# The first expert chosen on the chip, fewer places, and high-half products ahead of low ones

## The chip, the cores and the metric

The kernel runs on one core of one Trainium2 chip. The metric is the device time of one execution in microseconds (us). TensorE multiplies, VectorE and ScalarE convert and copy, GpSimd does some subtractions and indirect transfers, and SP issues the loads of weights to the core's 16 DMA engines. Each engine takes its instructions in program order.

## The reference

Two transformer layers over 512 tokens of width 1024: sliding-window attention with a dense SwiGLU, then forgetting attention with a mixture of eight experts, of which each token uses two. The stage that matters here:

```python
    logits = (x2 @ w_router).astype(jnp.float32) + b_router.astype(jnp.float32)
    top_vals, top_idx = lax.top_k(logits, TOP_K)
    gates = jax.nn.softmax(top_vals, axis=-1)
...
    def expert_block(args):
        xb, e = args
        h = xb @ w_in[e]
        return (jax.nn.silu(h[:, :D_FF]) * h[:, D_FF:]) @ w_out[e]
```

D_FF is 2816. An expert's weights are 1024 x 5632 and 2816 x 1024 numbers of 4 bytes, 34.6 MB; all eight are read once.

## The kernel before

**Weights.** The class `Weights` keeps a list of chunks of about 1 MB (128 x 2048 floats) in the order of use; an expert has 33, the last one 34. A chunk goes through three steps. `load` issues its DMA on SP into one of the raw buffers (three, and four "deep" ones once attention has given up its memory). `upper` lets ScalarE write its fp16 high half `wh` (L149), in two pieces of 1048 and 1000 columns. `lower` lets VectorE write the fp16 low half `wl` (L158) from the raw data and `wh`, after which the raw buffer is free and `load` goes on. Seven pairs of `wh` and `wl` exist; `free` says which were used up. `tick`, called between groups of matmuls, does a piece or two of each. `need` forces a chunk to be there. Every product is three matmuls: high weight by high data, high by low, low by high.

**Experts.** The kernel gives each of eight slots a fixed number of places, `CAP`. Slot 0 always has expert 0, whose weights can be loaded before anything is routed; the others are sorted by their tokens (`order_of`: `key`, `slot`, `ose`) and put on slots 1 to 7 by `TURN`, and SP reads their numbers from `eid` (`exp_of`, L296). A loop at the end (`nit`) serves tokens for which a slot has no place; `full` and `over` count whether there are any. A slot's places are the columns of its matmuls. `block4` computes four blocks of 128 hidden features for one unit of two chunks (L1442 to L1444), `quad` takes the products out, `gate_pair` does the last two blocks, `down_wide` the way down (L1471 to L1473); the last slot uses `down_direct`.

**Hand-over.** The last layer's attention ends with `finish`: four tiles of 128 tokens go through the output product, residual and norm. `aside(t, h, k)` hooks routing work between its matmuls: `route` computes a tile's logits, `ranks` the two best experts of each token, `places_of` each token's place in its expert's list and the one-hot lists of slot 0 (L1224), and `choose` gathers slot 0's token rows by matmuls of those one-hots (L1237, L1241). Of the last tile, `turn1` transposes the rows (L394), then `route`, `ranks`, `places_of` and `choose` follow, `chosen_to` copies the rows into `XA` (L231 on ScalarE, L1569 on VectorE) and slot 0 starts. Three chunks of expert 0 are loaded and converted during attention.

**Chores.** `small_work` is a list of small jobs: the lists of places (`lists`), the gates (`gates`, `gate_parts`) and a scaling of `xtok`. Each `tick` in slot 0 does one, from its first unit on.

## Time and profile before

| | us |
|---|---|
| median of three runs (1633.46 to 1636.43) | 1633.89 |
| the profiled execution | 1634.23 |
| its span, first to last instruction | 1632.4 |
| TensorE busy | 1578.6 |
| VectorE busy | 1210.9 |
| ScalarE busy | 950.3 |
| experts' first product at | 788.91 |

Times in the rows are counted from the start of the span. The view of the chain that ended last is no help in this kernel: it names only the last scatter. So the views read are the busy time of stretches, the waits, and the timeline.

### The profile page before, as it was taken

What the parts mean: (1) busy time and instruction counts of PE and PEld (TensorE: products, weight loads), DVE (VectorE), ACT (ScalarE), POOL (GpSimd) and SP (SyncE); (2) the same over time, 40 slices, a digit from 0 to 9 for tenths busy, and PEclk for the clock granted to TensorE, in tenths of its full rate; (3) what the DMA queues carried; (4) which work ended last, traced back from release to release, by engine and by line L of the source; (5) the groups of instructions that cost most, each with busy time, mean ns of one, the idle gap of its engine ahead of it and who ended that gap; (6) DMA issues with size and microseconds to landing.
All of it is one profiled execution on the core that took longest, in us unless ns stands there. A gap on an engine that the chain in (4) does not pass through costs nothing. (4 is left out here: it accounts for less than half of the span.)

```text
span 1632.4 us, 42978 instructions
## 1 busy us (share of the span) xinstructions
PE 1578.6 (97%) x18640; PEld 1267.8 (78%) x18640; DVE 1210.9 (74%) x1811; ACT 950.3 (58%) x1447; POOL 267.7 (16%) x264
## 2 busy tenths in 40 slices
PE   7998999999999999999899999999999999999996
PEld 6775654444444747765899999999999999999984
DVE  6798543333634568787898798888979889699997
ACT  6676243333211356663676787767877678666773
POOL 0443100000200000003120330203112030130251
PEclk9999999999999999999999999999999999999998
DMA  7511043332631132201899899999999999999993
GB/s 275 178 53 53 27 129 104 103 104 91 219 114 60 53 129 92 66 27 65 308 363 364 293 394 377 352 370 305 390 357 361 375 320 373 329 297 360 358 369 113
DMA packets 180549, 370.16 MB, mean 227 GB/s; under 512 B 6589, under 2 KB 49597, under 8 KB 180352
## 3 DMA queue, kind: packets, MB, share of 16 engines
q1 hardware_dynamic: 173280, 343.48, 58.6%
q0 software_dynamic: 4768, 15.47, 4.0%
q10 hardware_dynamic: 2304, 8.39, 1.4%
q8 instruction: 148, 2.42, 0.6%
q14 instruction: 49, 0.40, 0.1%
HBM read 355.08 MB, written 12.39 MB: 225 GB/s over the span
## 5 line engine op out<-in xcount | busy, mean ns | idle before, releaser
L158 DVE SCALAR_TENSOR_TENSOR wl<-raw,wh 128x1048 f16<-128x1048 f32 (+3 forms) x658 | 794.7, 1258 | 100.3 <-ACT wh L149 100.1
L149 ACT ACTIVATE wh<-raw 128x1048 f16<-128x1048 f32 (+3 forms) x658 | 641.8, 1036 | 101.7 <-PE bk L239 42.9
L1444 PE MATMUL bk<-xa,wl 128*128 128x160 f16 (+3 forms) x1280 | 260.0, 231 | 0.9 <-DVE wl L158 0.9
L1442 PE MATMUL bk<-xa,wh 128*128 128x160 f16 (+3 forms) x1280 | 260.1, 231 | 0.8 <-ACT xa L231 0.8
L1443 PE MATMUL bk<-xa,wh 128*128 128x160 f16 (+3 forms) x1280 | 260.0, 231 | 0.0
L1443 PEld LDWEIGHTS <-wh 128*128 128x128 f16 x2560 | 250.5, 98 | 3.6 <-issue 2.4
L1444 PEld LDWEIGHTS <-wl 128*128 128x128 f16 x2560 | 250.5, 98 | 1.3 <-DVE wl L158 1.1
L1442 PEld LDWEIGHTS <-wh 128*128 128x128 f16 x2560 | 250.4, 98 | 0.7
L1473 PE MATMUL bk<-act,wl 128*128 128x160 f16 (+6 forms) x1232 | 235.3, 227 | 1.2 <-DVE wl L158 1.2
L1472 PE MATMUL bk<-act,wh 128*128 128x160 f16 (+6 forms) x1232 | 235.3, 227 | 0.0
L1471 PE MATMUL bk<-act,wh 128*128 128x160 f16 (+6 forms) x1232 | 235.2, 227 | 0.0
L1442 PE MATMUL bk<-xe,wh 128*128 128x128 f16 (+2 forms) x1280 | 223.2, 221 | 2.2 <-DVE sa L1458 1.4
L1443 PE MATMUL bk<-xe,wh 128*128 128x128 f16 (+2 forms) x1280 | 223.1, 221 | 0.0
L1444 PE MATMUL bk<-xe,wl 128*128 128x128 f16 (+2 forms) x1280 | 223.1, 221 | 0.0
L237 PE MATMUL bk<-xTh,wh 128*128 128x512 f16 (+2 forms) x656 | 204.8, 322 | 1.2 <-DVE Kx L234 0.9
L239 PE MATMUL bk<-xTh,wl 128*128 128x512 f16 (+2 forms) x656 | 204.6, 322 | 1.4 <-DVE wl L158 1.4
L238 PE MATMUL bk<-xTl,wh 128*128 128x512 f16 (+2 forms) x656 | 204.6, 322 | 0.5 <-DVE xTl L234 0.5
L1460 POOL TENSOR_TENSOR act<-sa,act 128x512 f16<-128x512 f32 (+6 forms) x40 | 106.3, 2659 | 284.7 <-ACT act L231 284.6
L239 PEld LDWEIGHTS <-wl 128*128 128x128 f16 x944 | 92.4, 98 | 49.0 <-DVE wl L158 2.9
L237 PEld LDWEIGHTS <-wh 128*128 128x128 f16 x944 | 92.4, 98 | 48.7 <-ACT wh L149 2.0
L238 PEld LDWEIGHTS <-wh 128*128 128x128 f16 x944 | 92.5, 98 | 46.6 <-issue 1.5
L1473 PEld LDWEIGHTS <-wl 128*128 128x128 f16 x1232 | 120.5, 98 | 1.6 <-DVE wl L158 1.6
(349 smaller groups left out, 2669.2 us busy)
## 6 DMA issues: line engine op xcount, KB each, us to landing
raw<-in_w_exp_in_dram SPq DMA_DIRECT2D x176, 1024.0 KB
raw<-in_w_exp_out_dram SPq DMA_DIRECT2D x85, 1024.0 KB
raw<-in_w_ffn_in_dram SPq DMA_DIRECT2D x22, 1024.0 KB
raw<-in_w_out_dram SPq DMA_DIRECT2D x8, 1024.0 KB
raw<-in_w_ffn_out_dram SPq DMA_DIRECT2D x8, 1024.0 KB
raw<-in_w_in_fox_dram SPq DMA_DIRECT2D x8, 1024.0 KB
raw<-in_w_in_swa_dram SPq DMA_DIRECT2D x4, 896.0 KB
raw<-in_w_mem_kv_dram SPq DMA_DIRECT2D x3, 1024.0 KB
```

The source lines that it names most:

```text
L149: self.nc.scalar.activation(h[:, p:e], t[:, p:e], AF.Copy, scale=SW)
L158: self.nc.vector.scalar_tensor_tensor(l, src, SW, h, op0=OP.mult, op1=OP.subtract)
L237: nc.tensor.matmul(o, lh, rh, start=first, stop=False, **kw)
L238: nc.tensor.matmul(o, lh, rl, start=False, stop=False, **kw)
L239: nc.tensor.matmul(o, ll, rh, start=False, stop=last, **kw)
L1442: nc.tensor.matmul(o, wh[:, k, c], xe[0][:, k, :C], start=first, stop=False, skip_group_check=True)
L1443: nc.tensor.matmul(o, wh[:, k, c], xe[1][:, k, :C], start=False, stop=False, skip_group_check=True)
L1444: nc.tensor.matmul(o, wl[:, k, c], xe[0][:, k, :C], start=False, stop=k == KD - 1, skip_group_check=True)
L1460: lambda: nc.gpsimd.tensor_sub(act[1][:, j, :C], sa[:, :, :C], act[0][:, j, :C])]
L1471: nc.tensor.matmul(o, wh[:, k, c], act[0][:, kk, :C], start=first, stop=False, skip_group_check=True)
L1472: nc.tensor.matmul(o, wh[:, k, c], act[1][:, kk, :C], start=False, stop=False, skip_group_check=True)
L1473: nc.tensor.matmul(o, wl[:, k, c], act[0][:, kk, :C], start=False, stop=kk == KF - 1, skip_group_check=True)
```

## The change

Slot 0's expert is now chosen on the chip: after three of the four tiles are routed, `choice` counts their tokens, takes the expert with the second most (ties by number), and keeps its one-hot `oh0` and its number `e0i`. Expert loads are shut (`shut`) until then, and SP reads `e0i` ahead of the first. `CAP` falls by four in five slots. The one-hots of slot 0 need `oh0` and move to `first_list`, after the last tile's norm; `choose` moves behind it. Four pieces of `upper` are forced between `route` and the second part of `choose`. The first two units of slot 0 do all their products with high weights first (`passes` (0, 1), through `need_high`) and then those with low weights (2). `lists` runs at once, the other chores only from the fourth unit on (`calm`); the gates are split in two, and the count of tokens without a place becomes a chore (`beyond`). Lists and gates of slot 0 move to later units.

```diff
@@ -51,7 +51,7 @@
 PIECE = 1048
-CAP = [160, 128, 152, 134, 144, 140, 168, 128]
+CAP = [156, 128, 148, 130, 140, 136, 168, 128]
 TURN = [0, 6, 2, 5, 3, 4, 1, 7]
@@ -92,6 +92,7 @@
         self.piece = PIECE
+        self.shut = True
@@ -107,6 +108,8 @@
             i = self.dma - self.from_
+            if i >= 0 and self.shut:
+                return
             pool, back = self.raw, NRAW
@@ -173,6 +176,11 @@
+    def need_high(self, i):
+        while self.hcut <= i:
+            assert self.upper(True)
+        return self.chunks[i][3][0]
     def free(self, u, n=None):
@@ -289,11 +297,12 @@
-    expert = {0: 0}
+    expert = {}
...
         if s not in expert:
-            expert[s] = nc.sync.value_load(eid[0:1, s:s + 1], min_val=0, max_val=NEXP - 1)
+            row = eid[0:1, s:s + 1] if s else e0i[0:1, 0:1]
+            expert[s] = nc.sync.value_load(row, min_val=0, max_val=NEXP - 1)
         return exp_src(expert[s])[which]
@@ -355,7 +364,6 @@
         nc.vector.tensor_scalar(R["first"], R["iota8"], -1.0, None, op0=OP.mult)
-        nc.vector.memset(R["first"][:, 0:1], FAR * NEXP)
         R["room"] = base.tile([128, NEXP, NT], FT, name="room")
@@ -1169,6 +1177,10 @@
     selb = base.tile(V3, BF, name="selb")
+    oh0 = base.tile([128, NEXP], FT, name="oh0")
+    low0 = base.tile([128, 1], FT, name="low0")
+    e0i = base.tile([128, 1], I32, name="e0i")
+    pos0 = base.tile([128, NT], FT, name="pos0")
@@ -1211,6 +1223,21 @@
+    def choice(pb):
+        for i in range(NT - 1):
+            nc.tensor.matmul(pb[:, 64:64 + NEXP], ones, selb[:, i, :], start=i == 0, stop=i == NT - 2)
+        key0 = small.tile([128, NEXP], FT, name="key0")
+        nc.vector.scalar_tensor_tensor(key0, pb[:, 64:64 + NEXP], float(NEXP), iota8, op0=OP.mult, op1=OP.add)
+        most = small.tile([128, NEXP], FT, name="most")
+        nc.vector.max(out=most, in_=key0)
+        nc.vector.tensor_scalar(oh0, key0, most[:, 1:2], None, op0=OP.is_equal)
+        cross(key0, oh0, iota8, OP.mult)
+        nc.vector.tensor_reduce(low0, key0, axis=AX.X, op=OP.add)
+        nc.vector.tensor_copy(e0i, low0)
+        W.shut = False
+        W.load()
     def places_of(t0, t1, pb):
@@ -1220,8 +1247,15 @@
               pb[:, 32 + t0 * NEXP:32 + t1 * NEXP].rearrange("p (t e) -> p t e", e=NEXP), OP.add)
+    def first_list(t0, t1):
+        n = t1 - t0
+        own = small.tile([128, NT, NEXP], FT, name="own")[:, :n]
+        cross(own, posm[:, t0:t1], oh0[:, None, :].to_broadcast([128, n, NEXP]), OP.mult)
+        nc.vector.tensor_reduce(pos0[:, t0:t1], own, axis=AX.X, op=OP.add)
         for t in range(t0, t1):
-            nc.vector.tensor_scalar(oh_[0][:, t, :CAP[0]], iota_c[:, :CAP[0]], posm[:, t, 0:1], None, op0=OP.is_equal)
+            nc.vector.tensor_scalar(oh_[0][:, t, :CAP[0]], iota_c[:, :CAP[0]], pos0[:, t:t + 1], None, op0=OP.is_equal)
@@ -1268,10 +1302,11 @@
             oh_.append(op.tile([128, NT, CMAX], FH, name="PTh", bufs=2))
-            places_of(0, 3, bank())
+            pb3 = bank()
+            choice(pb3)
+            places_of(0, 3, pb3)
         if (t, h, k) == (3, 1, 15):
             xe_out.extend([bank2(), bank2(), bank()])
-            choose(range(0, 6), range(3))
@@ -1303,13 +1338,17 @@
     finish(u_o1, mixT, gb1, out_left, turn1, aside)
+    first_list(0, NT - 1)
     turn1(NT - 1)
-    choose(range(6, 11), range(3))
+    choose(range(0, 8), range(3))
     pb = bank()
     route(NT - 1, pb)
-    choose(range(11, 2 * KD), range(3))
+    for _ in range(4):
+        W.upper(True)
+    choose(range(8, 2 * KD), range(3))
     ranks(NT - 1, NT, *rank_tmp())
     places_of(NT - 1, NT, pb)
+    first_list(NT - 1, NT)
     for i in range(NT):
@@ -1430,22 +1469,24 @@
-    def block4(C, u, xe, b, tick):
-        wh, wl = unit(u, 512)
+    def block4(C, u, xe, b, tick, passes=(0, 1, 2)):
+        ws = unit(u, 512)
         for kk in (0, 4):
...
                 for k in range(kk, kk + 4):
-                    first = k == 0 and f % 2 == 0
-                    nc.tensor.matmul(o, wh[:, k, c], xe[0][:, k, :C], start=first, stop=False, skip_group_check=True)
-                    nc.tensor.matmul(o, wh[:, k, c], xe[1][:, k, :C], start=False, stop=False, skip_group_check=True)
-                    nc.tensor.matmul(o, wl[:, k, c], xe[0][:, k, :C], start=False, stop=k == KD - 1,
-                                     skip_group_check=True)
+                    for p in passes:
+                        if p < 2 and 2 not in passes:
+                            w = W.need_high(W.first[u] + kk // 4)[:, k % 4 * 512 + f * 128:k % 4 * 512 + f * 128 + 128]
+                        else:
+                            w = ws[p == 2][:, k, c]
+                        nc.tensor.matmul(o, w, xe[p == 1][:, k, :C], start=p == 0 and k == 0 and f % 2 == 0,
+                                         stop=p == 2 and k == KD - 1, skip_group_check=True)
                 if f % 2:
                     tick()
-            if kk == 0:
+            if kk == 0 and 2 in passes:
                 W.free(u, 1)
@@ -1551,13 +1592,17 @@
     tot = small_t("tot", [128, 1])
-    nc.vector.scalar_tensor_tensor(key, pb[:, 64:64 + NEXP], float(NEXP), first, op0=OP.mult, op1=OP.add)
-    nc.vector.max(out=top, in_=key)
-    cross(over, top[:, :, None].to_broadcast([128, NEXP, NT]), full, OP.is_gt)
-    nc.vector.tensor_reduce(tot, over.rearrange("p a b -> p (a b)"), axis=AX.X, op=OP.add)
-    nc.vector.tensor_copy(toti, tot)
+    def beyond():
+        nc.vector.max(out=top, in_=key)
+        cross(over, top[:, :, None].to_broadcast([128, NEXP, NT]), full, OP.is_gt)
+        nc.vector.tensor_reduce(tot, over.rearrange("p a b -> p (a b)"), axis=AX.X, op=OP.add)
+        nc.vector.tensor_copy(toti, tot)
     def order_of():
+        nc.vector.scalar_tensor_tensor(key, oh0, FAR * NEXP, first, op0=OP.mult, op1=OP.add)
+        nc.vector.scalar_tensor_tensor(key, pb[:, 64:64 + NEXP], float(NEXP), key, op0=OP.mult, op1=OP.add)
         nc.vector.tensor_copy(cnt, pb[:, 64:64 + NEXP])
@@ -1600,6 +1645,8 @@
         nc.scalar.activation(gt[:, 0], gt[:, 0], AF.Exp)
+    def gates_of():
         nc.vector.tensor_scalar(gt[:, 1], gt[:, 0], 1.0, None, op0=OP.add)
@@ -1622,11 +1669,14 @@
     def small_work():
-        lists()
-        yield
         gates()
         yield
+        yield
+        gates_of()
+        yield
         gate_parts()
+        yield
+        beyond()
         yield
@@ -1640,9 +1690,9 @@
     chores = small_work()
-    next(chores)
-    pend = []
+    lists()
+    pend, calm = [], []
@@ -1651,7 +1701,8 @@
             pend.pop(0)()
-        next(chores, None)
+        if calm:
+            next(chores, None)
         W.tick(1 if W.hcut >= W.done + LEAD else 2)
@@ -1737,27 +1788,35 @@
                     sa = mx.tile([128, 4, CMAX], FT, name="sa", bufs=2)
-                b = bank2()
-                block4(C, u, XE[s], b, tick)
+                if (s, i) == (0, 0):
+                    ahead = [bank2(), bank2()]
+                    for v, b in zip(u_ei[s], ahead):
+                        block4(C, v, XE[s], b, lambda: None, (0, 1))
+                if s == 0 and i < 2:
+                    b = ahead[i]
+                    block4(C, u, XE[s], b, tick, (2,))
+                else:
+                    b = bank2()
+                    block4(C, u, XE[s], b, tick)
                 rest = quad(C, b, i % 2, sa, act, i // 2)
...
             pend.extend(rest)
+            if (s, i) == (0, 3):
+                calm.append(True)
+            if (s, i) == (0, 9):
+                G[0] = own_gates(0, oh0_, bank())
             if (s, i) == (0, 2):
-                for _ in range(2):
-                    next(chores, None)
-                G[0] = own_gates(0, oh, bank())
-            if (s, i) == (0, 0):
-                oh = places(me, lambda t: posm[:, t, 0:1], CAP[0])
-            if (s, i) == (0, 1):
-                _, _, *at_[0] = fetch(me, oh, blocks(0), False)
+                oh0_ = places(me, lambda t: pos0[:, t:t + 1], CAP[0])
+            if (s, i) == (0, 3):
+                _, _, *at_[0] = fetch(me, oh0_, blocks(0), False)
             if s + 1 < NEXP:
...
                     rows, _, *at_[s + 1] = fetch(me, oh, blocks(s + 1))
-                if i == 6:
+                if i == (6 if s else 10):
                     G[s + 1] = own_gates(s + 1, oh, bank())
...
                     ready(s + 1, rows)

```

## Rows read from the trace of the kernel before

**Rows 1.** Stretch, us, each engine's busy us (instructions), clock, DMA share, GB/s

```profile
820.00:1500.00 680.00, 680.00 (x10688) 677.71 (x10686) 589.67 (x602) 495.45 (x588) 128.87 (x63) 1.00 0.99 352
...
1500.00:1600.00 100.00, 96.59 (x1427) 87.85 (x1425) 95.99 (x102) 75.23 (x90) 35.24 (x9) 1.00 1.03 360
```

**Rows 2.** TensorE's waits from 1500 us on: us in total, times, longest

```profile
PE bk L1518 <- DVE wl L158: 4.4, 3, 3.9
```

**Rows 3.** Timeline of the hand-over: start, us, engine, instruction, count [idle before]

```profile
779.86 0.33 PE L394 MATMUL bk<-identf,xtok 128*128 128x128 f32 x1 [2.46 <-DVE xtok L446]
...
782.47 0.27 PE L1237 MATMUL bk<-PTh,xTl 128*128 128x128 f16 x1
...
783.40 0.27 PE L1237 MATMUL bk<-PTh,xTl 128*128 128x128 f16 x1
...
787.50 1.09 ACT L231 ACTIVATE xa<-bk 128x512 f16<-128x512 f32 x2 [5.12 <-PE bk L1237]
...
788.91 0.23 PE L1442 MATMUL bk<-xa,wh 128*128 128x160 f16 x1 [0.79 <-ACT xa L231]
```

**Rows 4.** Busy time of stretches at the hand-over, columns as in the first group

```profile
780.00:784.00 4.00, 4.00 (x57) 3.64 (x57) 1.85 (x3) 2.07 (x4) 2.31 (x2) 0.57 1.05 395
...
788.10:827.20 39.10, 36.59 (x525) 35.71 (x523) 35.31 (x72) 30.93 (x36) 7.46 (x2) 1.00 0.90 318
...
799.00:806.00 7.00, 5.32 (x71) 4.64 (x69) 6.92 (x12) 6.97 (x8) 0.00 (x0) 1.00 0.61 200
```

**Rows 5.** Busy time of 20 us at 160 and at 128 places

```profile
860.00:880.00 20.00, 20.00 (x292) 20.00 (x290) 19.92 (x19) 15.71 (x18) 1.52 (x1) 1.00 0.96 352
...
960.00:980.00 20.00, 20.00 (x362) 20.00 (x360) 20.00 (x20) 18.05 (x22) 5.93 (x1) 1.00 1.03 403
```

**Rows 6.** Busy time of the first 15 us of the second slot

```profile
903.00:918.00 15.00, 15.00 (x256) 14.88 (x254) 9.25 (x9) 11.45 (x16) 1.72 (x2) 1.00 0.61 170
```

**Rows 7.** Timeline of VectorE at the hand-over

```profile
774.97 0.16 DVE L1162 TENSOR_TENSOR posm<-posm,bk 128x24 f32<-128x24 f32 x1
...
775.17 0.73 DVE L1224 TENSOR_SCALAR PTh<-iota_c,posm 128x160 f16<-128x160 f32 x3
...
786.62 0.17 DVE L1554 SCALAR_TENSOR_TENSOR key<-bk,first 128x8 f32<-128x8 f32 x1
...
786.82 0.17 DVE L1555 MAX8 top<-key 128x8 f32<-128x8 f32 x1
...
788.14 1.29 DVE L1569 TENSOR_SCALAR xa<-bk 128x512 f16<-128x512 f32 x2 [0.52 <-PE bk L1241]
...
789.35 0.15 DVE L1561 COPY cnt<-bk 128x8 f32<-128x8 f32 x1
...
791.85 0.42 DVE L1595 TENSOR_REDUCE posS<-g 128x32 f32<-128x256 f32 x1
...
799.41 4.62 DVE L158 SCALAR_TENSOR_TENSOR wl<-raw,wh 128x1000 f16<-128x1000 f32 x4
```

**Rows 8.** SP: expert numbers read (ns, min/median/max); issues of expert loads

```profile
L296 SPq TENSOR_LOAD <-eid x7: 269/281/569, 868.5 to 1489.8; - x7
...
754.71 0.37 SPq L122 DMA_DIRECT2D raw<-in_w_exp_in_dram  x1
...
775.83 6.92 SPq L122 DMA_DIRECT2D raw<-in_w_exp_in_dram  x6
```

**Rows 9.** Busy time of two us in which one chunk moves

```profile
758.00:760.00 2.00, 2.00 (x12) 1.07 (x11) 0.05 (x1) 0.00 (x0) 0.00 (x0) 1.00 0.58 226
```

**Rows 10.** Busy time on raw in attention: VectorE, ScalarE, clock, DMA, GB/s

```profile
690.00:735.00 45.00, 9.74 (x8) 7.12 (x7) 1.00 0.10 35
```

**Rows 11.** TensorE's waits for VectorE, 690 to 776 us: first and last of five

```profile
PE bk L542 <- DVE PTl L234: 1.1, 1, 1.1
...
PE bk L394 <- DVE xtok L446: 0.5, 1, 0.5
```

**Rows 12.** ScalarE's wait for loads, 812 to 1500 us

```profile
ACT wh L149 <- DMA raw<-in_w_exp_in_dram: 4.0, 4, 2.3
```

## The prediction

> **What bounds the kernel now.** I read the profile in this order: the busy time of whole stretches, the list of what TensorE waited for, the matmul count of single stretches, and then the timeline of the hand-over from attention to the experts. From 820 to 1500 us TensorE is busy for 680.00 of 680 us [rows 1], and the list of its waits from 812 to 1500 us is empty. Weights are always converted before they are asked for, so in this stage the end is set by how many places pass through TensorE. Only after 1500 us do waits of TensorE appear, above all 4.4 us for low halves at the very end [rows 2]; VectorE, 95.99 of 100 us busy there [rows 1], limits that piece together with TensorE. The start is a chain: TensorE stands still for 2.46 us until the last tile is normalised, transposes it, routes it, and reaches expert products at 788.91, after ScalarE's last copy of the chosen rows [rows 3]. In 799 to 806 us it is busy for 5.32 of 7 us [rows 4]: 1.7 us are lost to low halves that come late. So five places of the edit can show: the columns, the hand-over, the first low halves, the stream of weights, and what attention no longer carries.
>
> **Columns: less work on the path.** Five of the eight slots shrink by 4 places (160, 152, 134, 144, 140), 20 in all. One expert is 22 blocks of 8 rows of weights, twice, and 22 x 8 on the way down, three products each: 1584 matmuls, all of which have the places as columns. At 160 places 292 matmuls pass in 20 us, 68.5 ns each; at 128 places 362, 55.2 ns [rows 5]. That is 0.415 ns for each column, still falling at 128. 4 x 0.415 x 1584 = 2.63 us for a slot, **13.1 us** for five. Nothing hides behind it, since TensorE has no wait there. That VectorE and the stream can follow faster slots is shown by the second slot, which runs at 128 places already and without a wait; in its first 15 us VectorE is busy 9.25 us and the DMA engines 0.61 [rows 6]: both are held back by full buffers. The block count stays at two for the five, so no transfer or list goes away. Bounds: 13.1 us in full, or 10.5 if the first slot's part is eaten by its own start.
>
> The Trainium skill speaks against this step: "TensorE: Matmul & The Clock Gate", section "Back-to-back issue gap", gives a stream of weight loads and matmuls about 81 ns for each matmul at 128 columns, more than the plain streaming time. By that, slots of 128 to 160 places would all be at that floor and the 20 places would bring nothing. The trace disagrees: 55.2 ns, with loads between [rows 5].
>
> **Hand-over: four pieces, all on the chain.** (a) `choice` puts six small VectorE operations ahead of the last tile's residual, each about 0.2 us apart as 786.62 and 786.82 show [rows 7]: +1.2 us. The three one-hots that stood there (0.73 us, of which 0.65 before the next operation) go: -0.65. Net +0.55 on everything behind the normalisation.
>
> (b) The six columns of `choose` that filled TensorE's pause are now behind the transposes: 24 pairs of matmuls ahead of `route`, not 15. A pair took 0.133 us in 782.47 to 783.40 (7 pairs) [rows 3], where the granted clock was 0.57, so mostly the 1.2 GHz level, after the pause of 2.46 us [rows 4]. The pause grows to about 4.6 us, so I take the low level for all: 9 x 0.133 = 1.2, less 0.3 for the start of the first, which waits for the new one-hots anyway: +0.9. At the full clock it would be +0.6.
>
> (c) `first_list` makes two more operations before the last one-hot: +0.4.
>
> (d) The four forced `upper` stand on ScalarE ahead of its copies of the chosen rows. They need chunks 0 and 1. The choice is written at about 776.2. A read of an expert's number on SP takes 0.27 to 0.57 us [rows 8], and I take 1 us with the register steps behind it, so the first load goes out near 777.3. A lone chunk issued at 754.71 is still moving at 226 GB/s in 758 to 760 and near its end there [rows 8, 9]: some 5 us. Chunk 0 is there at 782, chunk 1, 1.05 MB later at the 395 GB/s of 780 to 784 [rows 4], at 785. Four conversions end at about 787.5; the copies, at 787.50 before [rows 3], are due at 789.4. Cost 0, but this is the thinnest cover: each us by which chunk 1 is later than 787 is paid in full, up to some 3 us. Queued behind these instructions on ScalarE are the copies and the loads of the two norm vectors, and TensorE waits for the copies. SP's other issues behind the new read are the deep chunks, which went out from 775.83 on [rows 8]; they are pushed by 2 to 3 us.
>
> Sum: first product at 788.9 + 1.85 = 790.8. Bounds +0.9 and +5.
>
> **First low halves.** Before, three chunks were loaded and converted during attention (9.74 us of VectorE, 7.12 of ScalarE in 690 to 735 [rows 10]). Now none is. The high-only passes give TensorE 128 products of 66.8 ns, 8.6 us, to 799.4 before it needs a low half. VectorE is free of the chosen rows at 788.14 + 1.29 + 1.85 = 791.2, does ordering and lists (789.35 to 792.27 before, 2.9 us, and two operations more for the key, 0.4), and needs 4.62 us for four pieces, two chunks [rows 7], so 9.2 for four chunks: 803.7. Low products of 4.3 us could end at 803.7 and end near 805. A second account, at the thirteenth chunk: VectorE was busy 35.31 us in 788.1 to 827.2, which ends with that chunk [rows 4]. It gets 6.9 more (three chunks) and 1.2 (`beyond` and one operation for the key, off an idle stretch before): 790.0 + 43.4 = 833.4; TensorE asks at 790.8 + 12 x 3.21 + 1.8 = 831.1. So 2.3 us are lost, against 1.7: **+0.6**. Bounds: -1.7 if the delayed chores fall into gaps, +4 if all their 5.6 us (22 small operations for the gates at 0.2, and 1.2 above) fall where VectorE is already late. From there it gains on TensorE, 2.3 us for a chunk against 3.2, and the later slots start with full buffers as before.
>
> **Attention.** The three chunks' 7 us on VectorE and 6 us on ScalarE leave a stretch in which TensorE is nearly always busy. Its waits for VectorE in 690 to 776 are five lines from 1.1 to 0.5 us, 4.0 in sum [rows 11], which bounds the gain; most stand behind the stretch or have other causes. I take -0.5, from -2 to 0. Edits at nothing: the order of the key, the moved list for the first slot, and its gates (0,9), all behind products.
>
> **Sum.** The profiled execution took 1634.2 us (its span 1632.4 and 1.8 around it), 0.3 above the median of 1633.9. -13.1 + 1.85 + 0.6 - 0.5 = -11.15: 1623.1 by the profiled execution, **1622.8** against the median. The end of the kernel moves rigidly with it: its loads, sums and norms all hang on earlier slots, and the seventh slot starts with full buffers before and after.
>
> **Rivals.**
> *The start is free.* The chores fall into gaps and the stall goes: -13.1 + 0.9 - 1.7 - 0.5 = -14.4, 1619.5. For it: high-only products cover 8.6 us. Against: VectorE's account.
> *The start is dear.* Chunk 1 is late by 3 us and the low halves cost 2.3 more than before: -13.1 + 4.85 + 2.3 - 0.5 = -6.45, 1627.5; with both upper bounds (5 and 4) in full -4.6, 1629.3. For it: in-order ScalarE. Against: the margin of 2 us between chunk 1 and the copies.
> *The stream becomes the bound, slower.* The DMA engines' share is 0.99 at 352 GB/s over 680 us [rows 1]. If that is all they give, the columns bring nothing and the stream's late start counts to the end. It starts with chunk 0 at 777.3 where it stood at chunk 4 at 775.83: 4 x 2.7 + 1.5 = 12.3, less 2.7 for the engines' idle share in 799 to 806 (0.61 of 7 us) [rows 4], less 0.5: +9, 1643. It decides once TensorE waits for landings before 1500. Against: 403 GB/s in 960 to 980 [rows 5]; about 359 would do; ScalarE waited for these loads 4.0 us in all between 812 and 1500 [rows 12].
> *The edit doesn't fit.* If the choice falls on the expert with the most tokens, 156 places may not hold them and the loop at the end runs: another expert's weights, at least 90 us, over 1720. Counting the reference's own routing, the first three tiles give 109 and 108 to the two largest, and the second ends with 133 of 512 tokens; all slots hold.
> *A floor for each matmul above 68 ns*, at which fewer columns bring nothing: the rest of the sum, +1.95, 1635.9. Against: 55.2 ns at 128 [rows 5]. The Trainium skill states such a floor in "TensorE: Matmul & The Clock Gate", "Back-to-back issue gap".
>
> **Chances.** Forecast 0.60 (own range 1620.5 to 1626), free start 0.15, dear start 0.14, stream 0.07, misfit 0.03, floor 0.01. About 0.2%, 3.3 us, is what a measurement can tell from no change. Faster: 0.60 + 0.15 + 0.10 of the dear start = 0.85; same 0.05 (the rest of it and part of the stream); slower 0.10. The range takes in the first three and rounds out to 1619 and 1630.5, 0.89 by these chances.
>
> **What would show it.** Right: matmul counts in 20 us rise with four places less; TensorE still has no wait for a landing in the middle; first product near 790.8, a loss of 2 to 3 us in the first slot. Wrong: the copies of the chosen rows begin long after TensorE's last choosing product (ScalarE stood at a chunk); waits of TensorE for low halves in the third to sixth slot; a tail longer from the seventh slot on than before; a loop at the end.

## The result, and the profile of the changed kernel

The change made the kernel slower: **1651.88 us** (median, 1650.63 to 1652.38) against 1634.74 (1633.46 to 1636.43) of the kernel before on the same chip, a ratio of 1.0103 with a 95% interval of 1.0086 to 1.0121. The forecast was 1622.8 with a range of 1619 to 1630.5. The profiled execution of the changed kernel took 1652.0 us (span 1650.2).

The same two long stretches as in [rows 1] (columns as there):

```profile
820.00:1500.00 680.00, 665.31 (x10564) 659.65 (x10563) 584.52 (x623) 500.21 (x590) 119.05 (x63) 0.99 0.99 349
1500.00:1600.00 100.00, 94.72 (x1504) 93.34 (x1501) 91.84 (x91) 68.40 (x79) 24.99 (x7) 0.98 0.97 332
```

TensorE, busy for 680.00 us before, is busy for 665.31 now and passes fewer matmuls (10564 against 10688), though each has fewer columns. VectorE is busy for less time than before, so it isn't short of time either. The waits of the changed kernel from 820 to 1640 us tell more (engine, what waited, for whom: us in total, times, longest); groups of GpSimd and others of less weight are left out:

```profile
DVE sa L1499 <- PE bk L1485: 52.0, 22, 7.1
ACT wh L152 <- DMA raw<-in_w_exp_in_dram: 43.5, 44, 8.0
...
DVE wl L161 <- ACT wh L152: 25.5, 11, 4.2
...
PE bk L1485 <- DVE wl L161: 16.6, 14, 7.1
```

VectorE's two of the kernel before, in the same stretch:

```profile
DVE wl L158 <- ACT wh L149: 75.0, 53, 6.3
DVE sa L1458 <- PE bk L1444: 11.9, 13, 1.8
```

`sa` is the product of a quad, which reads what TensorE has just summed; `wl` is a low half, which follows ScalarE's high half. Before, VectorE stood ahead of the work, at conversions not yet due. Now it stands behind it, at a product whose sum isn't there. ScalarE's waits for landings were 4.0 us between 812 and 1500 before [rows 12].

Where the time went, slot by slot (from the first product of a slot to that of the next, the last one to its last product; us, read from the traces' products):

| slot (places before, after) | first product | 1 (160, 156) | 2 (128) | 3 (152, 148) | 4 (134, 130) | 5 (144, 140) | 6 (140, 136) | 7 (168) | 8 (128) |
|---|---|---|---|---|---|---|---|---|---|
| before | 788.9 | 114.1 | 92.5 | 107.4 | 96.5 | 103.0 | 100.5 | 119.2 | 98.5 |
| changed | 791.6 | 119.3 | 94.6 | 104.8 | 94.0 | 100.7 | 98.6 | 132.0 | 102.9 |
| e1 (below) | 792.1 | 114.0 | 92.5 | 104.8 | 93.8 | 100.4 | 97.8 | 119.5 | 99.4 |
| e3 (below) | 789.5 | 111.9 | 92.5 | 104.8 | 93.8 | 100.4 | 97.8 | 118.7 | 98.6 |

The first products also carry a spread of whole executions. TensorE's transposes of the third tile, which come ahead of everything that the hand-over's edits move, start between 762.9 us (e8 below) and 767.4 (e5). Counted from those transposes the first product comes after 23.1 us before and in e3, 25.7 in e1 and 26.6 in the changed kernel.

The third slot of the changed kernel gains 2.6 us, which is the prediction's 2.63 for a slot. The loss sits in the first, second, seventh and eighth, and the second, seventh and eighth slots have the same places as before.

**What the order of the instructions says.** `Weights.upper` writes a piece's high half and puts the piece on a list, `lower` takes one from the list and writes its low half, and a `tick` of the expert stage does one of each. The change writes 8 high halves ahead of any low half: four at the end of attention, the rest for the high-first passes of the first two units. `need` works off the two that the first chunk wants, and from then on one goes on and one comes off, so the list hardly gets shorter. Counted in the order in which the kernels write their instructions, at the end of each unit of the first slot, as the last finished chunk, with the unit's first one as number 0 (a unit of four blocks has 2 chunks, 4 pieces):

| | high halves written to | low halves to | loads to | pieces waiting |
|---|---|---|---|---|
| before | 5 | 4 | 11 | 1 |
| changed | 5 | 2 | 9 | 6 (5 from the second slot on) |
| e1 | 5 | 4 | 11 | 1 |

Counted in the traces, 7 pieces of the units behind a quad stood ahead of its product in VectorE's queue before. In the changed kernel it is 2 in the first slot and 3 from the second on, of the 4 that the next unit has. All others stand behind the product. VectorE takes its queue in order, so it waits with ready work behind. The start of the seventh slot on VectorE (start, us, instruction [idle before <- released by]), changed kernel:

```profile
1411.06 1.25 DVE L161 SCALAR_TENSOR_TENSOR wl<-raw,wh 128x1048 f16<-128x1048 f32 x1 [4.21 <-ACT wh L152]
1419.45 0.86 DVE L1499 SCALAR_TENSOR_TENSOR sa<-bk,sa 128x672 f32<-128x672 f32 x1 [7.14 <-PE bk L1485]
1420.22 6.27 DVE L161 SCALAR_TENSOR_TENSOR wl<-raw,wh 128x1000 f16<-128x1000 f32 x4
```

For 7.14 us VectorE writes nothing, though ScalarE wrote three high halves in that time (1412.13, 1414.31 and 1416.49). The same place in e1, where only the list is worked off:

```profile
1405.19 1.20 DVE L162 SCALAR_TENSOR_TENSOR wl<-raw,wh 128x1000 f16<-128x1000 f32 x1 [0.89 <-ACT wh L153]
1407.39 1.25 DVE L162 SCALAR_TENSOR_TENSOR wl<-raw,wh 128x1048 f16<-128x1048 f32 x1 [1.01 <-ACT wh L153]
1409.53 1.20 DVE L162 SCALAR_TENSOR_TENSOR wl<-raw,wh 128x1000 f16<-128x1000 f32 x1 [0.89 <-ACT wh L153]
1411.11 1.25 DVE L162 SCALAR_TENSOR_TENSOR wl<-raw,wh 128x1048 f16<-128x1048 f32 x1 [0.38 <-ACT wh L153]
1412.28 0.85 DVE L1502 SCALAR_TENSOR_TENSOR sa<-bk,sa 128x672 f32<-128x672 f32 x1
```

The product has no wait here; the conversions that follow ScalarE piece by piece stand ahead of it. The Trainium skill says that the queues of ScalarE, VectorE and GpSimd are strictly first in, first out ("PSUM — Partial Sum Buffer", section "Engine vs sequencer instructions"); the 7.14 us agree with that.

From the sixth chunk on the chunks of the seventh slot are ready only 0 to 3 us before TensorE asks (7 to 10 in e1), and the first late transfer shows. ScalarE, VectorE and TensorE of the changed kernel:

```profile
1469.51 1.08 ACT L152 ACTIVATE wh<-raw 128x1048 f16<-128x1048 f32 x1 [8.02 <-DMA raw<-in_w_exp_in_dram]
```

```profile
1463.82 4.62 DVE L161 SCALAR_TENSOR_TENSOR wl<-raw,wh 128x1000 f16<-128x1000 f32 x4
1475.03 1.29 DVE L242 SCALAR_TENSOR_TENSOR xe<-bk,xe 128x512 f16<-128x512 f32 x2 [6.59 <-ACT xe L239]
```

```profile
1480.27 0.32 PE L1485 MATMUL bk<-xa,wl 128*128 128x168 f16 x1 [7.08 <-DVE wl L161]
```

A load issued at 1449.5 landed at 1469.4, while GpSimd's queue carried token sums (last section). ScalarE stood at it for 8.02 us, in front of the copy of `xe`; VectorE stood at its half of `xe` for 6.59, in front of the low half that TensorE wanted; TensorE stood for 7.08. The busy times of the 20 us with that wait and of the next 20 show what it costs beyond itself (columns as in [rows 1]):

```profile
1460.00:1480.00 20.00, 13.20 (x178) 12.98 (x176) 12.99 (x20) 11.13 (x14) 1.46 (x1) 0.90 1.04 339
1480.00:1500.00 20.00, 19.73 (x232) 19.63 (x233) 16.92 (x22) 11.37 (x14) 1.56 (x1) 0.84 0.81 280
```

After the pause TensorE's granted clock is 0.84 in the mean, so in part of the stretch its lower level: 232 matmuls pass in 20 us, where 275 do at 168 places at the full clock (e1, 1460 to 1480).

### The profile page after: what moved, and what is told of

It reads as the page before. It is cut to its first block, busy times and chain, and to the rows that moved or that the text cites. A ratio compares the mean times of both kernels' runs of the same rounds, so it can differ in the third digit from the quotient of the medians.

```text
span 1650.2 us, 43052 instructions
## 1 busy us (share of the span) xinstructions
PE 1575.8 (95%) x18643; PEld 1260.2 (76%) x18643; DVE 1211.6 (73%) x1821; ACT 956.6 (58%) x1448; POOL 245.2 (15%) x264
## 5 line engine op out<-in xcount | busy, mean ns | idle before, releaser
L161 DVE SCALAR_TENSOR_TENSOR wl<-raw,wh 128x1048 f16<-128x1048 f32 (+3 forms) x658 | 786.4, 1251 | 52.0 <-ACT wh L152 51.9
L1485 PEld LDWEIGHTS <-wh 128*128 128x128 f16 x5120 | 408.7, 98 | 2.0 <-DVE xa L1614 0.8
L1485 PE MATMUL bk<-xa,wl 128*128 128x156 f16 (+3 forms) x1280 | 250.0, 232 | 13.7 <-DVE wl L161 13.6
L1485 PE MATMUL bk<-xa,wh 128*128 128x156 f16 (+3 forms) x2560 | 258.0, 231 | 0.8 <-ACT xa L239 0.8
L1514 PE MATMUL bk<-act,wl 128*128 128x156 f16 (+6 forms) x1232 | 232.0, 227 | 2.2 <-DVE wl L161 2.2
L1512 PE MATMUL bk<-act,wh 128*128 128x156 f16 (+6 forms) x1232 | 231.9, 226 | 0.0
L1513 PE MATMUL bk<-act,wh 128*128 128x156 f16 (+6 forms) x1232 | 231.9, 226 | 0.0
L1485 PE MATMUL bk<-xe,wh 128*128 128x128 f16 (+2 forms) x2560 | 222.5, 220 | 0.0
L1501 POOL TENSOR_TENSOR act<-sa,act 128x512 f16<-128x512 f32 (+6 forms) x40 | 95.8, 2396 | 305.0 <-ACT act L239 304.9
L247 PEld LDWEIGHTS <-wl 128*128 128x128 f16 x944 | 92.5, 98 | 51.0 <-DVE wl L161 4.7
L245 PEld LDWEIGHTS <-wh 128*128 128x128 f16 x944 | 92.5, 98 | 48.3 <-ACT wh L152 1.6
L246 PEld LDWEIGHTS <-wh 128*128 128x128 f16 x944 | 92.5, 98 | 46.6 <-issue 1.5
L1513 PEld LDWEIGHTS <-wh 128*128 128x128 f16 x1232 | 121.0, 98 | 0.0
L1512 PEld LDWEIGHTS <-wh 128*128 128x128 f16 x1232 | 121.0, 98 | 0.0
L954 DVE SCALAR_TENSOR_TENSOR av<-bk,sa 128x512 f32<-128x512 f32 x22 | 15.2, 692 | 114.8 <-ACT sa L953 114.8
```

The costliest lines, as they stand in the source:

```text
L161: self.nc.vector.scalar_tensor_tensor(l, src, SW, h, op0=OP.mult, op1=OP.subtract)
L245: nc.tensor.matmul(o, lh, rh, start=first, stop=False, **kw)
L246: nc.tensor.matmul(o, lh, rl, start=False, stop=False, **kw)
L247: nc.tensor.matmul(o, ll, rh, start=False, stop=last, **kw)
L954: nc.vector.scalar_tensor_tensor(av, b[:, 1, :], DS * SA, sa, op0=OP.mult, op1=OP.mult)
L1485: nc.tensor.matmul(o, w, xe[p == 1][:, k, :C], start=p == 0 and k == 0 and f % 2 == 0, stop=p == 2 and k == KD - 1, skip_group_check=True)
```

## The experiments

Theory: the list of waiting pieces is what ate the columns. Rivals: the stream (late loads, the DMA engines), the delayed chores and the high-first order, and columns that bring less than reckoned. "Before" is each time the kernel before on the same chip, 1634.1 to 1634.4.

**e1, the changed kernel with the list worked off.**

```diff
             if self.wait and (len(self.wait) > LAG or not new):
                 self.lower()
+            if self.drain and len(self.wait) > LAG:   # drain: from the first slot on
+                self.lower()
```

> The changed kernel, and each tick of the expert stage writes a second low half while more than LAG = 1 pieces wait for theirs. As changed, the forced upper halves leave 6 pieces waiting, and since a tick takes one off for each it puts on, they wait in all eight slots: low halves stand one whole unit (4 pieces, 2 chunks) later in VectorE's order than before, and the loads behind them 2 chunks later. Backlog theory: this alone is what ate the columns; without it the sum of the prediction holds, 1623 (1619 to 1628), VectorE's waits at the quad product fall from 52 us to near the 12 of before, TensorE has no wait from 850 to 1500. Stream rival (the DMA engines, or the late start of the loads, set the end): 1645 to 1652 and waits for landings remain. Chores rival (the delayed routing work in slots 0 and 1 costs it): over 1640.

Measured: **1627.69** (1626.85 to 1628.11), ratio to before 0.9958 (0.9941 to 0.9975). These two lines give back 24.2 of the 29.1 us between forecast and result. VectorE's wait at `sa` is 7.5 us, and ScalarE's waits for landings are gone from the top of the list. All waits of TensorE from 780 to 1500 us in e1:

```profile
PE bk L405 <- DVE xtok L457: 4.1, 1, 4.1
PE bk L1488 <- DVE sa L1502: 1.6, 2, 1.3
PE bk L1488 <- DVE wl L162: 1.3, 3, 0.6
PE bk L1488 <- ACT sa L1501: 1.1, 2, 0.9
PE bk L1488 <- ACT xa L242: 0.8, 1, 0.8
PE bk L1274 <- DVE PTh L1261: 0.5, 1, 0.5
PE bk L1356 <- DVE posm L1173: 0.3, 1, 0.3
```

All of them lie before 880, and from the second to the sixth slot the lengths are those of e3. The stream carries this pace:

```profile
820.00:1500.00 680.00, 677.04 (x10818) 673.94 (x10815) 601.39 (x646) 505.40 (x599) 136.76 (x63) 1.00 1.01 359
```

359 GB/s, what the prediction had said would do, at nearly the same DMA share as the 352 of [rows 1].

**e2, e8, e9, the kernel before with nothing but the list.** From the first slot on a low half is written only when more than 6, 5 or 3 pieces wait (before: 1).

```diff
-            if self.wait and (len(self.wait) > LAG or not new):
+            if self.wait and (len(self.wait) > self.lag or not new):
...
     pend = []
+    W.lag = 6
```

> The kernel before with only the backlog: from the first slot on a tick writes a low half only when more than 6 pieces wait. Hand-over, columns, chores and preloaded chunks are as before. Backlog theory: what the change lost against the prediction, 1651.9 - 1622.8 = 29 us, is lost here too, less what the longer slots (13 us of columns) give VectorE: 1648 to 1664, with VectorE's waits at the quad product near 50 us. Stream and chores rivals: no change, 1633 to 1638.

> The kernel before with 5 pieces that wait for their low half where e2 had 6; 5 is what the changed kernel keeps from its second slot on (6 in its first). Backlog theory: the loss of the changed kernel against e1, 24.2 us, is found again on before: 1634.4 + 24 = 1658 (1650 to 1666). If only a sixth piece hurts and the changed kernel's loss is another: 1634 to 1640.

> The kernel before with 3 pieces that wait for their low half. A unit is 4 pieces, and 10 pieces (5 chunks) have their high half written ahead when a unit ends: with 1 waiting the low halves are written to the end of the next unit, with 3 to one piece short of it, with 5 not beyond the running unit's successor's start. If the loss grows with every piece in proportion (16 us at 5): 8 us, 1642. If it sets in only when a low half of the next unit stands behind the quad product that waits for TensorE, as the waits of e2 and e8 there say: 1633 to 1637.

Measured: 3 pieces **1642.0** (ratio 1.0051, 1.0031 to 1.0071), 5 pieces **1650.6** (1.0097, 1.0076 to 1.0119), 6 pieces **1699.6** (1.0400, 1.0383 to 1.0417). The list alone makes the kernel before slower, with nothing else of the change in it; the rivals said no change. The sizes were not foreseen: 3 was to cost nothing or 8 and cost 7.9; 5 was to cost 24 and cost 16; 6 was to cost 14 to 30 and cost 65. They come about in two ways. With 3 and 5 the slots from the first to the sixth keep their length within 0.8 us, and the loss is in the seventh (123.3 and 132.4 us against 119.2) and the eighth (102.0 and 102.2 against 98.5). With 6 every slot is 4.6 to 15.5 us longer. In the seventh and eighth slots together, 5 pieces lose 16.9 us on the kernel before and the change loses 16.0 against e1, so a list of this length by itself makes a loss of that size there. The change loses another 7.4 in its first two slots, where 5 pieces on the kernel before lose 0.3. The change has 6 waiting in its first slot; e2, with 6 throughout, loses 4.6 and 7.6 in these two. VectorE's and TensorE's waits of e2 (VectorE 820 to 1640, TensorE 780 to 1500):

```profile
DVE sa L1459 <- PE bk L1445: 91.8, 35, 13.1
```

```profile
PE bk L1445 <- DVE wl L159: 21.5, 32, 1.1
PE bk L240 <- DVE wl L159: 9.3, 12, 1.3
```

At a unit's end 12 pieces, counted from the unit's first, have their high half written (the expectation of e9 counts 10), and 4 are of the unit itself. By the traces 5 pieces of the next units stand ahead of the product with 3 waiting, 3 with 5 waiting and 2 with 6. With 6 the second chunk of the next unit is thus wholly behind the product, and TensorE waits at nearly every quad. That this one piece is the reason of the jump is read from the order and the 32 short waits; it wasn't varied further.

**e3, the kernel before with the new places.**

```diff
-CAP = [160, 128, 152, 134, 144, 140, 168, 128]
+CAP = [156, 128, 148, 130, 140, 136, 168, 128]
```

> The kernel before with the places of the changed one (156, 128, 148, 130, 140, 136, 168, 128), nothing else. By the prediction's column term, 13.1 us less: 1621.6 (1620 to 1623), TensorE still without a wait from 850 to 1500. If VectorE or the stream can't follow slots that are 3% shorter, less is gained: 1625 to 1634, and waits of TensorE for low halves appear.

Measured: **1621.54** (1619.91 to 1622.05), ratio 0.9919 (0.9903 to 0.9936), 12.9 us less. The column term was 13.1. It is the fastest kernel here, faster than before and than the change, and its first expert is still the fixed one. At 156 places 300 matmuls pass in the 20 us from 860 on, 66.7 ns each, 292 at 160 [rows 5]:

```profile
860.00:880.00 20.00, 20.00 (x300) 20.00 (x298) 20.00 (x19) 16.51 (x19) 1.50 (x1) 1.00 0.98 344
```

**e4, e1 with the places of before:** the start of the change alone.

> The changed kernel with the second low half for each tick, and the places of before (160, 128, 152, 134, 144, 140, 168, 128): the hand-over, the high-first start, the chores and attention alone. Backlog theory with the prediction's terms: 1634.7 + 1.85 + 0.6 - 0.5 = 1636.7 (1634 to 1640). Stream rival: as late as the changed kernel or later, 1650 and more. Chores rival: 1645 and more.

Measured: **1641.63** (1638.34 to 1642.13), ratio 1.0043 (1.0028 to 1.0057). 7.2 us over before, where e1 is 6.15 over e3. The start costs 6 to 7 us, not 1.95. It is 1.6 above the top of the theory's range and far from the stream's 1650.

**e5, e1 with two raw buffers less:** loads as late as in the change, VectorE's order as in e1.

```diff
-    W.widen(dp, NDEEP)
+    W.widen(dp, NDEEP - 2)
```

> e1 with 4 + 3 raw buffers cut to 2 + 3, so that a load is issued as late, counted in chunks, as in the changed kernel (9 chunks past the one TensorE has freed, not 11), while VectorE's order stays that of e1. It separates the two things that the backlog does. If low halves late in VectorE's order are what costs: 1627 to 1632, near e1's 1627.7. If it is the loads that start 2 chunks later, with ScalarE waiting for landings (43.5 us in the changed kernel): 1642 to 1652.

Measured: **1636.36** (1633.59 to 1639.60), ratio 1.0010 (0.9999 to 1.0021), 8.7 over e1: between the two expectations. So the list works in two ways. Loads two chunks later cost about a third of the 24.2 by themselves. That the low halves' place in VectorE's order stands for the rest is concluded, not measured, and the two needn't add up. In e5 VectorE waits 4.4 us at `sa`, and ScalarE waits for landings longer than in the changed kernel (820 to 1640):

```profile
ACT wh L153 <- DMA raw<-in_w_exp_in_dram: 77.1, 77, 5.9
```

The slots of e5 are those of e1 up to the sixth, within 0.3; the seventh takes 124.3 and the eighth 101.3 (119.5 and 99.4), 7.0 us in all. Its first product comes 1.9 later. Half of that, 1.0, is there already at the third tile's transposes and is the spread of executions. The other 0.9 arises at a lower granted clock, as in the changed kernel (hand-over, below).

**e6, e7, e10, the start taken apart.** e6 is e1 with the chores from the first tick on (`pend, calm = [], [True]`). e7 is e1 with every unit of the first slot as `b = bank2(); block4(C, u, XE[s], b, tick)`, without the passes ahead. e10 is e3 with

```diff
             i = self.dma - self.from_
+            if i >= 0 and self.shut:
+                return
...
+            W.shut = False
+            W.load()
             places_of(0, 3, bank())
...
+    for _ in range(4):
+        W.upper(True)
     choose(range(11, 2 * KD), range(3))
```

and the list worked off as in e1.

> e1 with the routing chores (gates, their parts, the bound) from the first tick on, not after the fourth unit. In e1 the first slot takes 114.0 us, 2.1 more than in e3; at 820 to 836 us ScalarE stands 5.1 us before the exponential of the gates, which VectorE reaches late in its order. Chores theory: in the first low halves they cost as much or less, first slot 112 to 114, total 1625.5 to 1628. If they are better late: they push the first low halves back, TensorE's wait of 1.3 us for low halves grows by their 5 us or so: 1629 to 1633.

> e1 with the first two units as all others: each step takes high, high and low product, none waits for the high ones of both units. The chunks still come as late as in the change. In e1 low halves of chunks 0 to 3 are done at 798.1, 800.4, 802.6 and 804.9, TensorE ends the two units at 805.9. Without the high-first order TensorE stands before the low product of chunk 0 until about 797 and then goes at its own pace, 3.2 us for a chunk: 797 + 13 = 810, 4 us later: 1631 to 1633. If the high-first order brings nothing (VectorE sets the pace either way): 1627 to 1629.

> e3 (kernel before, new places, first expert fixed) with the loads of the experts shut until the place where the changed kernel chooses, four forced upper halves ahead of ScalarE's copies, and the second low half for each tick. So the weights come as late as in the change, without the choice's operations, the moved one-hots and the high-first order. e1 is 6.1 us over e3. In the two traces 2.6 us of it arise before the first product (choice and one-hots), 2.1 in the first slot, 1.6 from the seventh on. If the late weights cost what the first slot lost: 1621.5 + 2 to 4 = 1623.5 to 1625.5, with the first product where e3 has it, 789.5. If the choice's operations are all of it: 1621.5. If the late weights are all of it: 1627.6.

Measured: e6 **1628.45** (ratio 0.9963, 0.9949 to 0.9977), e7 **1627.60** (0.9958, 0.9944 to 0.9972), e10 **1627.79** (0.9960, 0.9946 to 0.9974). Against e1, neither the late chores nor the high-first order moves the total by what can be measured. In the profiled executions the first slot takes 114.0 with both, 116.6 without the late chores, 116.1 without the high-first order, and 118.0 in e10 without either. So each is worth 2 to 2.6 us at that place, of which the totals don't show as much. e7's forecast of 4 us more is a miss.

e10 isn't what its expectation calls it. SyncE's queue waits for nothing where `load` was moved to, so it issued the first load at 679.3 as before; what became late is the conversion. (In the changed kernel SyncE has to read the chosen expert first, and the load goes out at 776.4.) Read that way it says something else: with first product at 789.0 and chunks in place long before, the first slot is 118.0, 6.1 longer than in e3, and the total is 6.25 over e3. Three chunks not converted ahead cost about 6 us without the other two measures.

**e11, e12, more lead on e3.** e11 is e3 with no waiting piece (`W.lag = 0`), e12 with `W.hcut >= W.done + LEAD + 2`.

> e3 with no piece waiting: from the first slot on each tick writes the low half of the piece whose high half it has just written. On the kernel before 3, 5 and 6 waiting pieces cost 8, 16 and 65 us. If that goes on below 1 in proportion (4 us for a piece): 1617.5. If 1 is already on the flat part, since TensorE has no wait for a low half between 850 and 1500 us in e3: 1620.5 to 1623; VectorE then only waits more for ScalarE.

> e3 with ticks of two until the high halves are 6 chunks ahead of TensorE, not 4: one whole unit more of lead, both halves. If lead is what the first slot and the tail of e3 still lack (about 2 and 6 us against the pitch of the middle slots): 1615 to 1619. If a unit ahead is enough and the first slot is held by VectorE's rate, which a longer lead doesn't change: 1620.5 to 1623; a longer lead could also push the quad's product behind more conversions: up to 1626.

Measured: e11 **1629.87** (1627.29 to 1633.84; 0.9976, 0.9966 to 0.9985), e12 **1622.73** (0.9932, 0.9916 to 0.9949). Neither is faster than e3. A list that is too short costs 8 us: VectorE then stands behind ScalarE for 96.7 us in 102 waits (69.0 in 51 in e3), and the seventh slot takes 122.7. I had expected e11 faster or equal. In e12's profiled execution the first slot is 3.9 us longer than in e3 and the last two are 3.2 shorter, so the longer lead moves time rather than saving it.

## Why the prediction was wrong, point by point

**What failed is the last sentence of the first low halves, "From there it gains on TensorE, 2.3 us for a chunk against 3.2, and the later slots start with full buffers as before"**, and with it "the end of the kernel moves rigidly". The rates are right and VectorE has the time, but it can't use it: a low half can't pass the product ahead of it in the queue, and the order is fixed by ticks that write one for one. The prediction costed the four forced high halves by ScalarE's time and by what is queued behind them there. It didn't ask what these four, and the four more of the high-first passes, leave on the list, which the diff and `tick` would have told without a trace. The list was put at nothing, and it cost 24.2 us (the change less e1).

**None of the rivals was this.** The stream came nearest, since it gave waits of TensorE for landings before 1500 as its sign and 1643 as its time. But e1 runs at the shorter places without those waits; the landings became late because the list held the raw buffers, and e5 prices that at 8.7. Of the signs of being wrong that the prediction named, one came clearly, the tail longer from the seventh slot on. The copies of the chosen rows weren't late, and TensorE's waits for low halves in the third to sixth slot were 0.5 us in two.

**Columns, 13.1: right.** The places alone gave 12.9 (e3), and 2.6 in the third slot. A matmul at 128 columns takes 55.2 ns [rows 5]. The Trainium skill's figure of about 81 ns for it ("TensorE: Matmul & The Clock Gate", section "Back-to-back issue gap") isn't met here, and that fewer columns would then bring nothing was the prediction's own reading of it.

**Hand-over, 1.85: 2.6 in e1, 3.5 in the change.** The traces of e3 and e1 happen to run alike up to 775 us, so the rows can be set side by side: VectorE in e3, then in e1.

```profile
776.45 0.41 DVE L423 SCALAR_TENSOR_TENSOR xtok<-xtok,bk 128x256 f32<-128x256 f32 x1
...
784.96 0.17 DVE L1181 SCALAR_TENSOR_TENSOR lg<-bk,br 128x8 f32<-128x8 f32 x1 [1.30 <-PE bk L239]
...
786.95 0.30 DVE L1224 TENSOR_SCALAR PTh<-iota_c,posm 128x156 f16<-128x156 f32 x1
```

```profile
777.49 0.42 DVE L434 SCALAR_TENSOR_TENSOR xtok<-xtok,bk 128x256 f32<-128x256 f32 x1 [0.57 <-PE bk L250]
...
786.91 0.17 DVE L1196 SCALAR_TENSOR_TENSOR lg<-bk,br 128x8 f32<-128x8 f32 x1 [1.81 <-PE bk L250]
...
789.56 0.30 DVE L1261 TENSOR_SCALAR PTh<-iota_c,pos 128x156 f16<-128x156 f32 x1
```

(a) The choice: 1.04 at the last residual, not 0.55. VectorE's own operations took what was reckoned, but it then waits 0.57 for TensorE, which had itself stood 0.76 for the key in the middle of its output products; this wait was not in the sum. (b) `choose` behind the transposes: at the logits 1.95 - 1.04 = 0.91, against 0.9. (c) `first_list`: 2.61 - 1.95 = 0.66, against 0.4. (d) The four forced high halves: 0, as said. ScalarE in the changed kernel is done with them at 786.65 and waits for TensorE before its copies:

```profile
782.76 3.89 ACT L152 ACTIVATE wh<-raw 128x1048 f16<-128x1048 f32 x4
790.21 1.08 ACT L239 ACTIVATE xa<-bk 128x512 f16<-128x512 f32 x2 [3.56 <-PE bk L1271]
```

The 0.9 that the changed kernel takes beyond e1's 2.6 goes with TensorE's clock. The same instructions stand there in both. In e1 the granted clock is full 4 us behind the last tile's transposes, in the changed kernel it is 0.69 in the mean, in part the lower level, and VectorE waits 2.60 us for the logits, not 1.81. First the stretch of e1, then the changed kernel's (columns as in [rows 1]), and its logits:

```profile
785.50:789.50 4.00, 3.66 (x100) 3.52 (x97) 1.91 (x11) 2.63 (x3) 0.00 (x0) 1.00 1.00 344
784.00:788.00 4.00, 4.00 (x93) 4.00 (x92) 1.45 (x8) 2.65 (x3) 0.00 (x0) 0.69 1.01 339
786.22 0.17 DVE L1193 SCALAR_TENSOR_TENSOR lg<-bk,br 128x8 f32<-128x8 f32 x1 [2.60 <-PE bk L247]
```

e5 has this 0.9 too (0.70), and e4, e6 and e7 don't. What decides it the runs don't show.

**First low halves, +0.6: 2.1 in e1, and more without its measures.** VectorE's account was good: the thirteenth chunk was to be done at 833.4, and in e1 it is at 833.6. TensorE reaches that chunk as far behind its first product as in e3 (42.5 us, 42.9 there). The 2.1 come in the two chunks behind it, where the delayed chores stand: the exponential of the gates makes ScalarE wait for VectorE. That the chores cost it is read from this place; with them early, in e6, the first slot is longer still.

```profile
827.94 0.20 ACT L1650 ACTIVATE gt<-gt 128x4 f32<-128x4 f32 x1 [5.10 <-DVE gt L1649]
```

The prediction had them as the bound of +4 and placed them nowhere.

**Attention, -0.5: nothing.** From TensorE's transposes near 544 us to those of the third tile near 766 it takes 222.15 us before and 222.14 in e3, 222.11 in the change and 222.09 in e1. That the three chunks are gone brings 0.05.

**The sum again:** -12.9 (e3) + 6.15 (start, e1 less e3) + 24.2 (list, with the clock's 0.9 of the profiled execution in it) = 17.4 by the medians; measured 17.1. 2.6 and 2.1 of the start are placed above. The other 1.6 are what e1's seventh and eighth slots take beyond e3's; e7's take only 0.2 more, so they are more likely the spread of single executions than a cost.

## What to carry to other kernels

Where conversions and loads are paced by a counter (one on, one off), a burst at the start may never be paid back: follow the counters through one round of the steady loop by hand before costing the burst by its own time. An in-order engine can be idle and late at once; its sign in the profile is an operation that has turned from waiting for its source to waiting for its consumer. Test one constant (here the places) apart from the larger edit that carries it: it had the whole gain.

## What the runs showed of the hardware that I had not expected

A load of 1 MB can be in flight for 20 to 23 us (issued 1449.5, landed 1469.4 in the changed kernel; 1436.4 and 1459.7 in e1) while GpSimd's queue carries token sums (`xtok<-expert_sums`, four transfers of 0.5 MB, landed by 1467.6 in the changed kernel). From 1456 to 1467 both queues together moved 236 GB/s. In 1456 to 1464 their packets are equal in number (columns of the queues: packets, MB, share of 16 engines):

```profile
q0 software_dynamic: 390, 1.41, 88.6%
q1 hardware_dynamic: 389, 0.40, 18.1%
```

The Trainium skill says that each DMA engine goes round robin between its queues ("DMA: Bandwidth & Descriptors", section "SWDGE vs HWDGE vs iDMA"); the two counts agree. Turns are not shares: GpSimd's packets carried 3.6 KB in the mean and the loads' 1.0 KB, since the rows of a `gate_pair` chunk are 256 numbers long. So the loads got about a fifth of the engines' time and moved 50 GB/s. The kernel before has such transfers too; it hid them behind the loads it had in advance, and this is where the shorter lead of the changed kernel cost most (12.5 of 24 us in the seventh slot).
